# Three more up pairs by two by two steps in phase two, over sums read back from DRAM

## The chip, the cores and the metric

One NeuronCore of a Trainium2 chip. The metric is the device time of one execution in microseconds, as the median of several runs.

## The reference

One layer of a streaming encoder over 512 positions of width 1024, float32, and a last RMSNorm. Only the channel mixer at the end matters here:

```python
h = rms_norm(x, norm_ffn_g)
up = causal_dwconv(h @ w_up, conv_ffn_w)      # 1024 -> 2 x 2816, three taps along the sequence
a, b = split(up, 2)
x = x + (silu(a) * b) @ w_down                # 2816 -> 1024
return rms_norm(x, norm_f_g)
```

Before it the layer computes the input projections, a gated short convolution, a forgetting attention, sigmoid gates (`gates`), and a product with `w_o` (Wo).

## The kernel before, in words

Everything lies transposed: features on the partitions, the 512 positions along the free axis. A product in full float32 is made of three passes: each operand is split into a high part (ScalarE copies into a reduced-precision type: `wh`, `gh`, `x1h`) and a low part (VectorE subtracts: `wl`, `gl`, `x1l`), and TensorE adds high x high, low x high and high x low. Weights come chunk by chunk through SP's queue in the order of the list `stream`; `split` makes the next chunk's two parts one chunk ahead, into two buffers each, so a split waits for TensorE's end of the chunk before the last.

The hidden width has 22 blocks of 128. A **pair** j is block j of `a` and block j of `b`. A plain pair is two products of 8 inner blocks x 2 halves of the positions x 3 passes, 96 matmuls of 256 columns. A pair in `SUP` goes **by two by two steps** (`seven`): the two outputs, two inner blocks and two halves of positions form two by two matrices, multiplied with seven products instead of eight. For each of the four q (two inner blocks each) there are a chunk P (three weight forms, from the host) and a chunk F (four forms). The weight sums of F are made in DRAM beforehand by `make_forms`: a copy on SP's queue, an accumulating DMA on GpSimd's, and so on in six stages, set off one by one by `slot()` calls. On the side of the positions, four sums per q are needed (`up_forms`): `scale` and `sums` make them in the tile `y` (one buffer, from pool `gx`), `parts_of` splits them into slots `XF` and on of `gh` and `gl`. In before they are made in the Wo stage, and used for pairs 1, 2 and 5. `merge` puts the seven products together on VectorE. `up_form` hands TensorE the operands: g < 3 are parts of x, the others are forms; the chunk P already uses one form.

The mixer runs in two phases (`PHASES`): up pairs 0 to 11, then the down product over these (`STEPS[0]`, by two by two steps too, over `gh`/`gl` slots given by `place`), then pairs 12 to 21 and `STEPS[1]`, then a plain remainder and the tail (`fin_out`). `glu` multiplies the finished pair: `ge` (even j) and `go` (odd j) on GpSimd. `taps` is the convolution: one ScalarE operation and two on VectorE, into a tile `fu`. PSUM has eight banks; the output pair 2 of the down product stays open in four of them from phase one to the end of phase two (`HELD`). Short VectorE and ScalarE works are put in the list `later` and set between splits by `run_later` with a budget in microseconds, or forced by `flush`. Matmuls, DMAs and a few others keep the order in which the code is written; the rest is set by a scheduler.

Of the kernel before, what the change touches and what calls it, by code (L numbers as in the profile page):

```python
# [8 lines left out]
F32 = mybir.dt.float32  # L9
# [4 lines left out]
P = 128  # L14
D = 1024
S = 512
# [36 lines left out]
)  # L53
HELD = 2

# [5 lines left out]

SUP = (1, 2, 5)
XF = 26
UPD = tuple(((j, q), (j, q + 1)) for j in SUP for q in (0, 2))
DOUBLES = GATES + UPD + STEPS[0] + STEPS[1]
N0 = len(GATES) + len(UPD)
GROUPS = {"gate": (2, 4, 1), "up": (2, 4, 1), 0: (2, 4, 1), 1: (2, 3, 1)}


@with_exitstack  # L70
def block_kernel(ctx, tc, xT, vecs, wv, win, wmix, wo, wup, wst, wdp, outT):
# [70 lines left out]
    for ph, (j0, j1) in enumerate(PHASES):  # L142
        for j in range(j0, j1):
            if j in SUP:
# [44 lines left out]

    def make_forms(n0, n1, key):  # L190

        size, step, shift = GROUPS[key]
        make_forms.slot = 0
        cuts = [n0]
        for n in range(n0 + 1, n1 + 1):
            if n == n1 or n - cuts[-1] == size or len(DOUBLES[n]) != len(DOUBLES[cuts[-1]]):
                cuts.append(n)
        for g, (a, b) in enumerate(zip(cuts, cuts[1:])):
            m = len(DOUBLES[a]) * P
            f = dr.tile([P, b - a, 4 * m], F32, tag=f"f{a}", name=f"f{a}")  # L200
            w = wst[a:b].rearrange("n p c -> p n c")
            x0, x1, x2 = w[:, :, 3 * m : 5 * m], w[:, :, 5 * m : 7 * m], w[:, :, 7 * m : 8 * m]
            for n in range(a, b):
                made[n] = f[:, n - a, :]

            def put(dst, src):
                return lambda: keep(nc.sync.dma_start(dst, src))

            def add(dst, src):
                return lambda: keep(nc.gpsimd.dma_start(dst, src, accum_op=ALU.add))  # L210
# [3 lines left out]
            todo_bg.extend((make_forms.slot + step * k + shift * g, op) for k, op in enumerate(ops))  # L214
        todo_bg.sort(key=lambda w: w[0])
# [36 lines left out]
    def split(hl=None):  # L252
# [31 lines left out]
        if any(("e",) in w[2] for w in later):  # L284
            run_later(k, {"u": 3.8, "P": 1.6, "F": 1.2}[nm[0]])
            return
# [498 lines left out]

    def seven(doubles, n0, sets, operand, goes_on=None, stays=None, done=None, of="q"):

# [13 lines left out]
        for n, (name, prods) in enumerate(todo):  # L801
# [5 lines left out]
            for c, i, (xh, xl), b, h in prods:  # L807
                if i not in open_:
# [4 lines left out]
                    open_[i][b][:, th[h]], (i, b), wh[:, cs], wl[:, cs], xh, xl,  # L813
                    (i, b) not in before and i != goes_on, (i, b) not in after and i != stays,
                ))
            passes(out, len(out))
            if name[0] == "F":
                for i in sorted({i for _, i, *_ in prods}):
                    if (i, 0) not in after and i != stays:
                        done(i, open_.pop(i), sets[i])  # L820
# [217 lines left out]

    def up_forms(q):

        y = gx.tile([P, 4, 2 * P], F32, tag="y", name=f"y{q}")
        b11, b12, b21, b22 = (y[:, i, :] for i in range(4))
        fs = slice(XF + 4 * q, XF + 4 * q + 4)

# [9 lines left out]
        def sums():  # L1054
            nc.vector.scalar_tensor_tensor(b22, b11, -1.0, b22, op0=ALU.mult, op1=ALU.subtract)
            nc.vector.scalar_tensor_tensor(b21, b22, -1.0, b21, op0=ALU.mult, op1=ALU.subtract)

        def parts_of():
            nc.scalar.activation(gh[:, fs, :], y, AF.Copy)
            nc.vector.tensor_sub(gl[:, fs, :], y, gh.bitcast(F32)[:, fs, :])  # L1060
# [4 lines left out]
    def up_form(q, g):  # L1065
# [3 lines left out]
        n = XF + 4 * q + (0, 3, 1, 2)[g - 3]  # L1069
        return gh[:, n, :], gl[:, n, :]  # L1070

    po = None
    make_forms(N0, N0 + len(STEPS[0]), 0)
    for j in range(KB):
# [11 lines left out]
        if j % 2:  # L1086
            up_forms(j // 2)
    hg.close()
# [17 lines left out]

    acc = turns(0, 1, *(2, 3, 4, 5) * 2, 6, 7, 0, 1, 2, 3, 4, 5)
    USETS = {1: (2, 3, 4, 5), 2: (6, 7, 0, 1), 5: (6, 7, 0, 1)}
    ssq3 = xp.tile([P, S], F32, tag="ssq", name="ssq3")

    def place(ph, q):
        return (q - PHASES[ph][0] // 2) * (NF + ph)

    def up(j, ph, rb2, pu=None):
# [6 lines left out]

        if j in SUP:
            c = len(GATES) + 2 * SUP.index(j)
            slot()
            seven(
                UPD[c - len(GATES) :][:2], c, {j: USETS[j]}, up_form, of="x",
                done=lambda i, banks, ids: merge(ph, j, banks, ids, rb2, tap, uu),
# [163 lines left out]
    for ph, (j0, j1) in enumerate(PHASES):  # L1291
        if ph:
            flush()
            acc = turns(*X * 5)
        if ph:
            make_forms(N0 + len(STEPS[0]), len(DOUBLES), ph)
        for j in range(j0, j1):
# [14 lines left out]
        seven(  # L1312
            STEPS[ph], N0 + ph * len(STEPS[0]), ({0: X, 1: Y, 3: X, 2: Y}, {0: X, 1: Y, 2: Y})[ph],
            lambda q, g: (gh[:, place(ph, q) + g, :], gl[:, place(ph, q) + g, :]),
            goes_on=HELD if ph == 1 else None, stays=HELD if ph == 0 else None,
            done=lambda i, banks, ids: combine(ph, i, banks, ids),
# [59 lines left out]
    def fin_out(t, rc):  # L1376
        hs = halves[t]
        pb = rstd_bc(rc, 2, (1, 5)[t], f"n3{t}")[:, : S // 2]
        rs = fp.tile([P, S], F32, tag="fu", name=f"rs{t}", bufs=3)[:, : S // 2]
        nc.scalar.activation(rs, pb, AF.Copy)  # L1380
        for g, (a, b) in enumerate(((0, 1), (1, 3), (6, 8), (3, 5), (5, 6))):
            y = x1[:, a:b, hs]
            eng, r = (nc.gpsimd, rs) if g == 2 else (nc.vector, pb)
            eng.tensor_mul(y, y, r.unsqueeze(1).to_broadcast([P, b - a, S // 2]))  # L1384
            keep((nc.sync, nc.scalar)[g % 2].dma_start(outT[:, a:b, hs], y))
# [30 lines left out]
def _layout(i):  # L1416
# [45 lines left out]
    wu4 = wup.reshape(2 * NP, P, KB, P)  # L1462
    for w4, d in [(wga, d) for d in GATES] + [(wu4, d) for d in UPD] + [(wdn, d) for d in STEPS[0] + STEPS[1]]:
        def pick(*which):
# [44 lines left out]
```

## Time and profile before

| | us |
|---|---|
| median of 3 runs (lowest to highest) | 697.87 (697.65 to 698.26) |
| the profiled execution's own time | 698.61 |
| its span | 696.8 |
| TensorE busy | 686.7 (99%) |
| VectorE, ScalarE, GpSimd busy | 530.9, 359.7, 180.7 |

The page gives the busy time of each engine, the chain of work that ended last, and the costliest groups. In the timeline a row is start, duration, engine, line, operation, and in brackets the idle time before it with what ended it. The up pairs of phase one begin at 340.6 us, the down steps of phase one at 471, phase two at 527.4, its down steps at 636.2.

### The profile page before, as it was taken

The numbers are of one execution on the slowest core, as the hardware profiler recorded it, in microseconds if no ns is written. First come the engines' busy times: TensorE is split into PE (matmuls) and PEld (weight loads), VectorE is DVE, ScalarE is ACT, GpSimd is POOL, SyncE is SP. The second block draws the span as 40 slices with busy tenths as digits, with TensorE's granted clock in tenths as the row PEclk, the third lists the DMA queues.
The fourth block names the chain that finished last, engine by engine and source line by source line (L and its number), as shares of the span: only waits on it lengthen the run. The fifth ranks groups of instructions, "written<-read, shape, count | busy, mean of one in ns | idle before, by whom it ended". The sixth has DMA issues, their size and how long they took to land.

```text
span 696.8 us, 14636 instructions
## 1 busy us (share of the span) xinstructions
PE 686.7 (99%) x5972; PEld 684.9 (98%) x5972; DVE 530.9 (76%) x824; ACT 359.7 (52%) x567; POOL 180.7 (26%) x196
## 2 busy tenths in 40 slices
PE   9999999999999999999999999999999999999996
PEld 9999999999999998999999999999999999999995
DVE  6677877776678776868869799988674677878793
ACT  5665655645565443446554455465443344445572
POOL 4134847532211201113523143210000313221001
PEclk9999999999999999999999999999999999999998
DMA  7528978542688687666799775536646686676513
GB/s 253 161 70 276 205 183 201 121 91 89 234 237 257 183 234 208 202 216 141 110 316 296 199 184 130 153 124 193 198 129 228 143 192 162 184 170 175 156 31 121
DMA packets 58387, 124.68 MB, mean 179 GB/s; under 512 B 5280, under 2 KB 26800, under 8 KB 58320
## 3 DMA queue, kind: packets, MB, share of 16 engines
q1 hardware_dynamic: 40776, 99.68, 44.0%
q0 software_dynamic: 16304, 22.88, 20.6%
q10 hardware_dynamic: 1240, 1.19, 0.5%
q8 instruction: 47, 0.77, 0.4%
q14 instruction: 20, 0.16, 0.1%
HBM read 121.57 MB, written 39.32 MB: 231 GB/s over the span
## 4 chain that ended last, share of the span: by engine, by line
PE 58%; DVE 2%; DMA 0%; ACT 0%; issue 0%; DVEq 0%; ACTq 0%
PE p_up L308 21%; PE dn L326 19%; PE p_up L326 7%; PE p_wo L308 6%; PE pdB L308 1%; PE pdA L308 1%; PE ya L308 1%; PE yc L308 1%; DMA raw_dp<-in_wdp_dram 0%; PE pc_n L343 0%; DVE fu L562 0%; DVE fu L565 0%; PE pb_n L362 0%; DVE gl L1231 0%; DVE wl_up L278 0%; DVE x L1384 0%
## 5 line engine op out<-in xcount | busy, mean ns | idle before, releaser
L308 PE MATMUL p_up<-x1h,wh_up 128*128 128x256 f32 x464 | 90.5, 276 | 0.0
L308 PE MATMUL p_up<-x1l,wh_up 128*128 128x256 f32 x464 | 90.3, 276 | 0.0
L308 PE MATMUL p_up<-x1h,wl_up 128*128 128x256 f32 x464 | 90.3, 276 | 0.0
L210 POOL DMA_DIRECT2D f<-in_wst_dram x57 | 66.1, 1311 | 15.6 <-DMA f<-f 15.3
L308 PEld LDWEIGHTS p_up<-x1h,wh_up 128*128 128x128 f32 x464 | 69.9, 188 | 0.0
L308 PEld LDWEIGHTS p_up<-x1l,wh_up 128*128 128x128 f32 x464 | 69.9, 188 | 0.0
L308 PEld LDWEIGHTS p_up<-x1h,wl_up 128*128 128x128 f32 x464 | 69.8, 188 | 0.0
L274 ACT ACTIVATE wh_up<-raw_up 128x1024 fp32r<-128x1024 f32 x38 | 40.2, 1058 | 55.8 <-PE p_up L308 46.2
L278 DVE TENSOR_TENSOR wl_F<-raw_F,wh_F 128x1024 fp32r<-128x1024 f32 (+1 forms) x36 | 46.9, 1304 | 17.8 <-ACT wh_F L274 17.8
L278 DVE TENSOR_TENSOR wl_up<-raw_up,wh_up 128x1024 fp32r<-128x1024 f32 x38 | 48.3, 1270 | 12.8 <-ACT wh_up L274 12.7
L308 PE MATMUL p_in<-xgh,wh_in 128*128 128x256 f32 x288 | 56.8, 279 | 0.0
L308 PE MATMUL p_in<-xgh,wl_in 128*128 128x256 f32 x288 | 56.6, 278 | 0.0
L308 PE MATMUL p_in<-xgl,wh_in 128*128 128x256 f32 x288 | 56.5, 278 | 0.0
L274 ACT ACTIVATE wh_F<-raw_F 128x1024 fp32r<-128x1024 f32 (+1 forms) x36 | 37.9, 1052 | 34.1 <-PE dn L326 26.6
L1204 POOL TENSOR_TENSOR ge<-fu,fu 128x512 f32<-128x512 f32 x11 | 17.6, 1602 | 138.6 <-DVE fu L565 119.1
L274 ACT ACTIVATE wh_P<-raw_P 128x768 fp32r<-128x768 f32 (+1 forms) x36 | 30.0, 834 | 31.4 <-PE dn L326 22.6
L308 PEld LDWEIGHTS p_in<-xgh,wh_in 128*128 128x128 f32 x288 | 44.7, 188 | 0.7
L326 PE MATMUL dn<-gh,wh_F 128*128 128x256 f32 x192 | 45.1, 276 | 0.0
L326 PE MATMUL dn<-gl,wh_F 128*128 128x256 f32 x192 | 45.1, 276 | 0.0
L278 DVE TENSOR_TENSOR wl_P<-raw_P,wh_P 128x768 fp32r<-128x768 f32 (+1 forms) x36 | 34.5, 958 | 13.6 <-ACT wh_P L274 9.0
L308 PEld LDWEIGHTS p_in<-xgl,wh_in 128*128 128x128 f32 x288 | 43.7, 188 | 0.0
L308 PEld LDWEIGHTS p_in<-xgh,wl_in 128*128 128x128 f32 x288 | 43.6, 188 | 0.0
(351 smaller groups left out, 2154.8 us busy)
## 6 DMA issues: line engine op xcount, KB each, us to landing
raw_up<-in_wup_dram SPq DMA_DIRECT2D x38, 512.0 KB, 3.9
raw_F<-f SPq DMA_DIRECT2D x35, 512.0 KB, 4.9
raw_P<-in_wst_dram SPq DMA_DIRECT2D x35, 384.0 KB, 4.7
raw_in<-in_win_dram SPq DMA_DIRECT2D x26, 512.0 KB, 3.5
f<-in_wst_dram POOLq DMA_DIRECT2D x35, 256.0 KB, 6.4
f<-in_wst_dram SPq DMA_DIRECT2D x17, 512.0 KB, 5.5
f<-in_wst_dram POOLq DMA_DIRECT2D x17, 512.0 KB, 8.1
f<-f SPq DMA_DIRECT2D x34, 256.0 KB, 5.6
```

What stands on the lines that cost most here:

```text
L210: return lambda: keep(nc.gpsimd.dma_start(dst, src, accum_op=ALU.add))
L274: ins = nc.scalar.activation(hi, raw, AF.Copy)
L278: ins = nc.vector.tensor_sub(lo, raw, hi.bitcast(F32))
L308: keep(nc.tensor.matmul(out[:, cs], w, x[:, cs], start=start and i == 0 and c == 0, stop=stop and i == 2 and c == len(cut) - 1,))
L326: keep(nc.tensor.matmul(out, wl if x == 1 else wh, xl if x == 2 else xh, start=opens and bk not in seen, stop=closes and bk not in left,))
L1204: keep(nc.gpsimd.tensor_mul(ge, a.rearrange(halves_of, h=2), b.rearrange(halves_of, h=2)))
```

## The change

- `SUP` holds the pairs of each phase: 1, 3, 5 in phase one (1, 2, 5 before), and 14, 16, 18 in phase two (none before). Their banks are always 2 to 5 (`USET`).
- `up_forms(q, 0)` writes each `y` to the DRAM tile `ys` as well, on GpSimd's queue. `up_forms(0, 1)`, at the start of phase two, loads `y` back; its `parts_of` calls `up_forms(q + 1, 1)`, so the four loads follow each other through the one buffer `y`.
- Pair 2 of the down product isn't held in PSUM: it is added into `x1` at the end of each phase, and `seven` loses `goes_on` and `stays`.
- `make_forms` takes a start, and the forms of the new pairs are made in phase one. In the gates stage the three `slot()` calls of an iteration stand together at its beginning. `place` gives other slots in phase two. The last up block of each phase calls `split_next()` once. The budget "u" is 4.2 instead of 3.8.
- The tail multiplies all output blocks on VectorE; ScalarE's copy `rs` and GpSimd's share go.

```diff
-SUP = (1, 2, 5)
-XF = 26
+SUP = ((1, 3, 5), (14, 16, 18))
+XF = (26, 0)
...
-                    (i, b) not in before and i != goes_on, (i, b) not in after and i != stays,
+                    (i, b) not in before, (i, b) not in after,
...
-    make_forms(len(GATES), N0, "up")
+    make_forms(NU[0], ND[0], "up0")
     for j in range(KB):
         gs = []
-        slot()
+        for _ in range(3):
+            slot()
...
         for pp, hh, ll, o in ((yc, ych, ycl, 0), (ya, oth, otl, 4)):
-            slot()
...
-    def up_forms(q):
-
-        y = gx.tile([P, 4, 2 * P], F32, tag="y", name=f"y{q}")
+    ys = dr.tile([4, P, 4, 2 * P], F32, tag="ys", name="ys")
+
+    def up_forms(q, ph):
+
+        y = gx.tile([P, 4, 2 * P], F32, tag="y", name=f"y{ph}{q}")
...
+            keep(nc.gpsimd.dma_start(ys[q], y))
+
         def parts_of():
             nc.scalar.activation(gh[:, fs, :], y, AF.Copy)
             nc.vector.tensor_sub(gl[:, fs, :], y, gh.bitcast(F32)[:, fs, :])
-
+            if ph and q < 3:
+                up_forms(q + 1, ph)
+
+        if ph:
+            keep(nc.gpsimd.dma_start(y, ys[q]))
+            later.append((len(parts) + 1, 1.25, (("x", q),), parts_of))
+            return
...
+    make_forms(NU[1], ND[1], "up1", 10)
...
-    acc = turns(0, 1, *(2, 3, 4, 5) * 2, 6, 7, 0, 1, 2, 3, 4, 5)
-    USETS = {1: (2, 3, 4, 5), 2: (6, 7, 0, 1), 5: (6, 7, 0, 1)}
+    acc = turns(0, 1, 6, 7, 0, 1, 6, 7, 0, 1, 2, 3, 6, 7, 0, 1, 2, 3)
+    USET = (2, 3, 4, 5)
...
+            if i and j + 1 == PHASES[ph][1]:
+                split_next()
...
         if ph:
-            flush()
-            acc = turns(*X * 5)
-        if ph:
-            make_forms(N0 + len(STEPS[0]), len(DOUBLES), ph)
+            acc = turns(6, 7, 0, 1, 6, 7, 0, 1, 6, 7, 0, 1, 6, 7)
+            up_forms(0, 1)
+            make_forms(ND[1], len(DOUBLES), ph)
...
-        rs = fp.tile([P, S], F32, tag="fu", name=f"rs{t}", bufs=3)[:, : S // 2]
-        nc.scalar.activation(rs, pb, AF.Copy)
-        for g, (a, b) in enumerate(((0, 1), (1, 3), (6, 8), (3, 5), (5, 6))):
+        for g, (a, b) in enumerate(((0, 1), (1, 3), (3, 5), (5, 7), (7, 8))):
```

GpSimd's queue in the gates stage, before and then now. `ga` is the sum of the two gated branches of an output block, `f10` to `f14` are the weight forms of the up pairs of phase one.

```order
L977 TENSOR_TENSOR ga4_3349<-ga4_3349,gb4_3354 128x512
L210 DMA f14_2593<-in_wst_dram 256x1x256
L977 TENSOR_TENSOR ga5_3538<-ga5_3538,gb5_3543 128x512
L210 DMA f10_2591<-in_wst_dram 256x1x256
L977 TENSOR_TENSOR ga6_3728<-ga6_3728,gb6_3733 128x512
```

```order
L978 TENSOR_TENSOR ga4_3351<-ga4_3351,gb4_3356 128x512
L978 TENSOR_TENSOR ga5_3540<-ga5_3540,gb5_3545 128x512
L211 DMA f10_2591<-in_wst_dram 256x1x256
L978 TENSOR_TENSOR ga6_3729<-ga6_3729,gb6_3734 128x512
L211 DMA f12_2592<-in_wst_dram 256x1x256
```

The accumulating DMA of `f14` stood ahead of `ga5` and now stands behind it.

GpSimd's queue at the start of phase two, before and then now. `ge6` and `go6` are the products of pairs 12 and 13, `f28` (before) and `f34` (now) are the first weight forms of phase two's down steps, and `y10` to `y13` are the four sums loaded back, the second digit being q.

```order
L1204 TENSOR_TENSOR ge5_6099<-fu100_6088,fu101_6094 128x512
L1204 TENSOR_TENSOR ge6_7007<-fu120_6940,fu121_7002 128x512
L210 DMA f28_6883<-in_wst_dram 256x1x512
L1211 TENSOR_TENSOR go6_7135<-fu130_7067,fu131_7130 128x512
L210 DMA f30_6884<-in_wst_dram 256x1x512
```

```order
L1218 TENSOR_TENSOR ge5_6068<-fu100_6057,fu101_6063 128x512
L1070 DMA y10_6913<-ys_4002 128x1024
L1218 TENSOR_TENSOR ge6_7045<-fu120_6972,fu121_7040 128x512
L211 DMA f34_6915<-in_wst_dram 256x1x512
L1070 DMA y11_7123<-ys_4002 128x1024
L1225 TENSOR_TENSOR go6_7181<-fu130_7109,fu131_7176 128x512
L211 DMA f36_6916<-in_wst_dram 256x1x512
L1070 DMA y12_7193<-ys_4002 128x1024
L1070 DMA y13_7263<-ys_4002 128x1024
```

The loads of y11 and y12 stand behind the products of pairs 12 and 13, and y13 right behind y12.

VectorE at the same place, before and then now: `fz121` is the evacuation of pair 12's second half, the rows into `fu121` its two taps, `wl` the low parts of weights.

```order
L1139 TENSOR_TENSOR fz121_7000<-p_up25_6951,rb_n2_4669 128x512
L278 TENSOR_TENSOR wl_up27_7076<-raw_up27_6849,wh_up27_7075 128x1024
L562 SCALAR_TENSOR_TENSOR fu121_7002<-fz121_7000,vec_64,fu121_7002 128x511
L565 SCALAR_TENSOR_TENSOR fu121_7002<-fz121_7000,vec_64,fu121_7002 128x510
L1139 TENSOR_TENSOR fz130_7065<-p_up26_7016,rb_n2_4669 128x512
L278 TENSOR_TENSOR wl_up28_7142<-raw_up28_6945,wh_up28_7141 128x1024
```

```order
L1153 TENSOR_TENSOR fz121_7038<-p_up25_6989,rb_n2_4675 128x512
L279 TENSOR_TENSOR wl_up27_7118<-raw_up27_6875,wh_up27_7117 128x1024
L563 SCALAR_TENSOR_TENSOR fu121_7040<-fz121_7038,vec_64,fu121_7040 128x511
L1065 TENSOR_TENSOR gl_3998<-y10_6913,gh_3997 128x1024
L566 SCALAR_TENSOR_TENSOR fu121_7040<-fz121_7038,vec_64,fu121_7040 128x510
L1153 TENSOR_TENSOR fz130_7107<-p_up26_7058,rb_n2_4675 128x512
L279 TENSOR_TENSOR wl_P28_7188<-raw_P28_6977,wh_P28_7187 128x768
L563 SCALAR_TENSOR_TENSOR fu130_7109<-fz130_7107,vec_64,fu130_7109 128x511
L566 SCALAR_TENSOR_TENSOR fu130_7109<-fz130_7107,vec_64,fu130_7109 128x510
L1065 TENSOR_TENSOR gl_3998<-y11_7123,gh_3997 128x1024
```

The split of y10 into `gl` stands between the two taps, that of y11 behind the taps of pair 13's first half. On TensorE the chunk P of pair 14 is now six products of three matmuls: x in the first four of each q's group, the form in the last two, so the low part of y11 is read by the twelfth matmul of the first chunk, and that of y12 and y13 by the sixth and the twelfth of the second.

More of the change, by code (lines that the diff above doesn't have):

```diff
@@ L60 @@
 PCUTS = (0, 8, 12, 20)
[L62 to L67 removed]
+SUP = ((1, 3, 5), (14, 16, 18))
+XF = (26, 0)
+UPD = tuple(tuple(((j, q), (j, q + 1)) for j in js for q in (0, 2)) for js in SUP)
+DOUBLES = GATES + UPD[0] + STEPS[0] + UPD[1] + STEPS[1]
+NU = [len(GATES), len(GATES + UPD[0] + STEPS[0])]
+ND = [NU[i] + len(UPD[i]) for i in range(2)]
+GROUPS = {"gate": (2, 4, 1), "up0": (2, 4, 1), "up1": (2, 3, 1), 0: (2, 4, 1), 1: (2, 3, 1)}
 @with_exitstack
@@ L188, in block_kernel, with make_forms @@
     made, todo_bg = {}, []
-    def make_forms(n0, n1, key):
+    def make_forms(n0, n1, key, start=0):
         size, step, shift = GROUPS[key]
-        make_forms.slot = 0
+        if not start:
+            make_forms.slot = 0
         cuts = [n0]
@@ L213, in make_forms @@
             ops = (put(f0, x0), add(f0, x1), put(f1, f[:, :, :m]), add(f1, x1[:, :, m:]), put(f2, f1), add(f2, x2))
-            todo_bg.extend((make_forms.slot + step * k + shift * g, op) for k, op in enumerate(ops))
+            todo_bg.extend((start + step * k + shift * g, op) for k, op in enumerate(ops))
         todo_bg.sort(key=lambda w: w[0])
@@ L818, in seven @@
                 for i in sorted({i for _, i, *_ in prods}):
-                    if (i, 0) not in after and i != stays:
+                    if (i, 0) not in after:
                         done(i, open_.pop(i), sets[i])
```

33 lines of the change are left out of this document (15 added, 18 removed).

## The prediction

> **What bounds the kernel now.** I read the page first, then TensorE's table of waits, then the chain that ended last.
>
> ```profile
> span 696.8 us, 14636 instructions
> PE 686.7 (99%) x5972; PEld 684.9 (98%) x5972; DVE 530.9 (76%) x824; ACT 359.7 (52%) x567; POOL 180.7 (26%) x196
> ```
>
> TensorE is busy for all but 10.1 us of its span. Its table of waits (who was waited for: us in total, times, longest) names 3.5 of these; most of the rest is the tail after the last matmul.
>
> ```profile
> PE dn L326 <- ACT wh_P L274: 1.6, 1, 1.6
> PE warm L115 <- DVE ones L107: 1.1, 1, 1.1
> PE dn L326 <- DVE wl_P L278: 0.8, 1, 0.8
> ```
>
> In the chain (start, us, what) a plain up block is 48 matmuls in 1.36 + 4.08 = 5.44 us:
>
> ```profile
> 527.39 1.36 PE p_up L326 x12
> 528.75 4.08 PE p_up L308 x36
> ```
>
> So a matmul of 256 columns costs 4.08/36 = 0.1133 us, and a matmul saved is time saved, but any new wait of TensorE adds to the time in full.
>
> **Part 1: fewer matmuls, -4.08 us.** A plain pair has 96 matmuls, a pair by two by two steps 84 (4 blocks of inner dimension x 7 products x 3). Three more such pairs save 36, x 0.1133 = 4.08 us. Moving the three of phase one from 1, 2, 5 to 1, 3, 5 changes no count; ending pair 2's sum in phase one changes none either. It adds a second `combine` on VectorE, six operations no wider than the 512 columns of a tap (0.74, below), so 4.4 us at most, beside pairs 12 and 13, where VectorE was busy for 11.2 of 21.6 us (a window's row: length, then PE, PEld, DVE, ACT and POOL busy, granted clock, DMA share, GB/s); without that cover they would delay the splits by as much.
>
> ```profile
> 527.40:549.00 21.60, 21.60 (x193) 21.60 (x193) 11.21 (x13) 6.48 (x9) 2.29 (x2) 1.00 0.62 163
> ```
>
> **Part 2: two old waits go, -1.55 and -0.78 us.** The first lies in the gates stage (timeline rows of POOL, ACT and PE):
>
> ```profile
> 267.84 1.04 POOL L210 DMA_DIRECT2D f<-in_wst_dram  x1 [15.29 <-DMA f<-f]
> 268.44 1.76 POOL L977 TENSOR_TENSOR ga<-ga,gb 128x512 f32<-128x512 f32 x1
> 270.24 0.63 ACT L978 ACTIVATE mh<-ga 128x512 fp32r<-128x512 f32 x1 [3.75 <-POOL ga L977]
> 270.77 0.83 ACT L274 ACTIVATE wh_P<-raw_P 128x768 fp32r<-128x768 f32 x1
> 271.65 0.38 PE L326 MATMUL dn<-xgh,wh_P 128*128 128x256 f32 x1 [1.55 <-ACT wh_P L274]
> ```
>
> GpSimd's queue stands 15 us at an accumulating DMA whose input copy has not landed; `ga5` is behind it, ScalarE's `mh` behind that, and the next weight split behind `mh`. In the new order `ga5` stands ahead of that DMA, so I take the whole 1.55 us as gone (bounds: 0, if another transfer takes its place, to 1.55). The second is the split of the first down chunk, which VectorE does only after the last `gl`:
>
> ```profile
> 469.12 1.28 DVE L1231 TENSOR_TENSOR gl<-go,gh 128x512 fp32r<-128x512 f32 x2
> 470.32 0.95 DVE L278 TENSOR_TENSOR wl_P<-raw_P,wh_P 128x768 fp32r<-128x768 f32 x1
> ```
>
> The added `split_next()` puts this split ahead of the `gl` rows; the 0.8 us go (bounds 0 to 0.8).
>
> **Part 3: the sums kept in DRAM, +20.7 us.** Writing `ys` in the Wo stage lies beside TensorE: the next `scale` may start about a microsecond late, and blocks there are 5.44 us long with a split made one block ahead. Reading them back is another matter. All four pass through the one buffer `y`: load, ScalarE's copy into `gh`, VectorE's difference into `gl`, and only then the next load. Prices of a hop: four 512 KB loads from GpSimd (issue ns min/median/max, then us to landing), and the two splits of the same tile in the Wo stage:
>
> ```profile
> L856 POOL DMA_DIRECT2D xt<-in_xT_dram x4: 555/559/639, 185.7 to 187.4; - x4
> DMA to landing us min/median/max: 4.9/6.1/7.5
> L1059 ACT ACTIVATE gh<-y x4: 1062/1062/1063, 313.5 to 346.5; 128x1024 fp32r<-128x1024 f32 x4
> L1060 DVE TENSOR_TENSOR gl<-y,gh x4: 1224/1226/1226, 314.6 to 347.6; 128x1024 fp32r<-128x1024 f32 x4
> ```
>
> No row shows such a load alone on the queue; I take 5.5 us to landing, between the burst's first and its median, since an accumulating transfer goes ahead of two of them (bounds below). A hop is then 5.5 + 1.06 + 1.23 = 7.8 us, and three follow the first. Where they start is read from the same place of before, the first pairs of phase two; t counts from TensorE's start of pair 12, 527.39:
>
> ```profile
> 538.31 1.06 ACT L274 ACTIVATE wh_up<-raw_up 128x1024 fp32r<-128x1024 f32 x1 [0.95 <-PE p_up L308]
> 539.40 1.23 DVE L278 TENSOR_TENSOR wl_up<-raw_up,wh_up 128x1024 fp32r<-128x1024 f32 x1 [0.40 <-ACT wh_up L274]
> 540.54 0.74 DVE L562 SCALAR_TENSOR_TENSOR fu<-fz,vec,fu 128x511 f32<-128x511 f32 x1
> 539.27 0.71 ACT L561 ACTIVATE fu<-fz,vec 128x512 f32<-128x512 f32 x1
> 542.25 1.29 POOL L1204 TENSOR_TENSOR ge<-fu,fu 128x512 f32<-128x512 f32 x1 [75.93 <-DVE fu L565]
> 543.48 1.06 POOL L210 DMA_DIRECT2D f<-in_wst_dram  x1
> ```
>
> The first tap of pair 12's second half starts at t = 13.15. In the new order VectorE makes the first `gl` (y10) between the two taps, done at 13.15 + 0.7 + 1.2 = 15.0, and the second tap at 15.8; GpSimd's `ge6`, at 14.9 before, waits for it. The load of y11 stands behind `ge6` (1.23 to the next start) and the accumulation of f34 (1.06): issued at 18.1, landed 23.6, `gl` done 25.9. Pair 14 begins at 4 x 5.44 = 21.76, and its first chunk already needs y11 in its twelfth matmul, at 23.0: **2.9 us wait**.
>
> The chunk ends at 26.7 (7 matmuls more). ScalarE's split of the next P chunk waits for it (0.83), then comes the tap of pair 13's second half (0.71), then on VectorE a tap, a split and the last tap (0.74, 0.95, 0.74): 30.6. GpSimd's `go6` needs that tap (1.29, as `ge`), then f36 (1.06), and only behind both stands the load of y12: issued 32.9, landed 38.4, `gl` done 40.7. TensorE has done its F chunk (24 matmuls, 2.7) by 29.4 and needs y12's low part at 30.0: **10.7 us wait**. The load of y13 waits for that `gl`: landed 46.2, `gl` done 48.5, while TensorE wants it six matmuls after y12, at 41.4: **7.1 us wait**. Together 20.7. Behind VectorE's and ScalarE's waiting instructions stand the splits of pair 15's weights; TensorE wants them only 31 matmuls (3.5 us) later, and they take 1.06 + 1.23, so nothing is added; behind the load of y13 on GpSimd's queue stand only three accumulations for phase two's steps and `ge7`, which comes after pair 14.
>
> At landings of 4.9 the sum falls by 1.8, at 7.5 it rises by 6. A 512 KB load from SP, another queue, has a median of 3.9 on the page:
>
> ```profile
> raw_up<-in_wup_dram SPq DMA_DIRECT2D x38, 512.0 KB, 3.9
> f<-in_wst_dram POOLq DMA_DIRECT2D x17, 512.0 KB, 8.1
> ```
>
> That is a lower end, 3 x 1.6 = 4.8 less. The Trainium skill, "DMA: Bandwidth & Descriptors", "Anatomy of one DMA — SWDGE (gpsimd) path", gives 2.0 us plus bytes/436e3 per DMA, an estimate of 3.2 for 512 KB, by which the 20.7 would be 13.8; the burst's fastest, 4.9, speaks against it here.
>
> **Part 4: TensorE's clock after the long waits, +2.0 us.** The granted clock (third from the end of a window's row) falls soon after the last matmul:
>
> ```profile
> 689.57 0.61 PE L362 MATMUL pb_n<-ident,rc_n 128*128 128x128 f32 x4
> 691.50:692.00 0.50, 0.00 (x0) 0.00 (x0) 0.50 (x2) 0.00 (x0) 0.50 (x1) 1.00 0.03 10
> 692.00:692.50 0.50, 0.00 (x0) 0.00 (x0) 0.50 (x2) 0.00 (x0) 0.01 (x1) 0.69 0.72 252
> 692.50:693.00 0.50, 0.00 (x0) 0.00 (x0) 0.15 (x1) 0.00 (x0) 0.00 (x0) 0.50 0.66 219
> ```
>
> Two microseconds idle and it is at half. At the span's start, two matmuls of 256 columns take 0.43 us from 5.50 to the next start, twice the 0.23 of later; the rate is reached at about 5.9:
>
> ```profile
> 1.05 4.21 PE L115 MATMUL warm<-ones 128*128 128x128 f32 x18 [1.05 <-DVE ones L107]
> 5.50 0.63 PE L474 MATMUL pb<-wh_v,xgh 128*128 128x256 f32 x2
> 5.93 0.49 PE L472 MATMUL pa<-wh_v,xgh 128*128 128x264 f32 x2
> ```
>
> From 1.05 to 5.9 are 4.8 us at half speed, 2.4 lost; the wait for y13 hides what is lost before it, so the loss counts once. I take 2.0 (bounds 0 to 2.4). "TensorE: Matmul & The Clock Gate", "What's actually happening", in the Trainium skill puts the way back at about 3.4 us of work, which would make it 1.7.
>
> **Part 5: the tail, +0.2 us.**
>
> ```profile
> 690.28 0.38 ACT L1380 ACTIVATE rs<-pb_n 128x256 f32<-128x256 f32 x1 [1.06 <-PE pb_n L362]
> 690.70 1.95 DVE L1384 TENSOR_TENSOR x<-x,pb_n 128x256 f32<-128x256 f32 x4 [1.28 <-ACT rs L1380]
> ```
>
> VectorE starts 0.4 sooner (no `rs`), but multiplies 8 blocks instead of 6: 1.95/6 x 2 = 0.65 more. The last output goes 0.2 later (bounds -0.4 to +0.65).
>
> **The sum** against the profiled execution's own 698.61: - 4.08 - 1.55 - 0.78 + 20.7 + 2.0 + 0.2 = 715.1. The median shown, 697.87, lies 0.74 under it: 714.4.
>
> **The rivals.**
> Loads land soon (chance 0.17): alone on the queue they need what SP's need, 3.9 us. 714.4 - 4.8 = 709.6, and 707.6 if the clock isn't lost. For it: the 4.9 comes from a burst of four. Against: y11 and y12 follow accumulations.
> Loads land late (0.13): y11 and y12 queue behind transfers that took 8.1 in the median, and y13 meets pair 15's weights: 7.5 each, 714.4 + 6 = 720.4.
> The loads are hidden (0.05), the side of faster: all land before they are needed, and the time is 714.4 - 22.7 = 691.7. The point from which it decides: from y10's `gl` (t = 15.0) to y13's need without waits (4 x 5.44 + 4.76 + 1.25 = 27.8) are 12.8 us for three hops, so 4.3 each and at most 2.0 to landing, even if GpSimd's `go6` were not in between. No 512 KB row is near that.
> VectorE becomes the bound in phase two (0.05): pairs by steps want more of it, and it would lag through pairs 15 to 19. The densest stretches of phase one speak against it (DVE is the third busy time):
>
> ```profile
> 373.00:394.00 21.00, 21.00 (x188) 21.00 (x187) 17.40 (x27) 8.25 (x13) 7.79 (x7) 1.00 1.03 265
> 416.00:438.00 22.00, 22.00 (x197) 22.00 (x196) 21.77 (x35) 12.62 (x20) 5.53 (x4) 1.00 0.62 135
> ```
>
> Even at 21.8 of 22 us TensorE never waited there. If it did, some 1 us per step pair: 714.4 + 3 = 717.4.
>
> **How the numbers follow.** The forecast of 714.4 has 0.60. The range goes from 705.5 (early landings, 707.6, and 2 us less for splits that overlap better than counted) to 721.5 (late landings and 1 us of other waits); it leaves out the hidden case and the far ends. A difference within 0.2% (about what a measurement of this kernel can tell from no change) lies between the hidden case and the rest, where no case is: 0.01. Faster 0.05, slower 0.94.
>
> **What would show it.** Right: TensorE's waits list `dn` in pair 14 behind `gl` of line 1065, two or three waits of 3, 11 and 7 us; GpSimd's `y` loads start at t = 18, 33 and 41; 36 fewer matmuls; no 1.6 us wait for `wh_P` at the gates. Wrong: TensorE unbroken through pair 14, or `y` loads landing within 2 us.

## The result, and the profile after

The changed kernel takes 738.31 us in the median (737.07 to 740.97, four runs) against 697.88: a ratio of 1.0577 [1.0557, 1.0598]. Slower, as forecast, but 24 us over the forecast of 714.4 and outside its range. The profiled execution has 738.93 us and a span of 737.1, 40.3 more than before.

The page (engine, busy time, instructions; then the granted clock in 40 slices):

```profile
span 737.1 us, 14705 instructions
PE 696.3 (94%) x5936; PEld 692.3 (94%) x5936; DVE 553.4 (75%) x858; ACT 369.4 (50%) x579; POOL 194.3 (26%) x211
PEclk9999999999999999999899999999997689999998
```

The 36 matmuls are gone (5972 to 5936), and yet TensorE is busy 9.6 us longer: about 13.7 us of its busy time are matmuls at a low clock (9.6 and the 4.1 of the 36). TensorE's waits in the changed kernel:

```profile
PE dn L327 <- ACT gh L1064: 21.6, 3, 11.0
PE pc_n L344 <- POOL ssq L1003: 3.0, 1, 3.0
PE p_up L327 <- ACT wh_up L275: 2.8, 1, 2.8
PE dn L327 <- DVE wl_F L279: 2.5, 1, 2.5
PE dn L327 <- DVE gl L1065: 2.0, 3, 0.7
...
PE p_up L309 <- DVE wl_up L279: 0.8, 1, 0.8
PE dn L327 <- ACT wh_F L275: 0.7, 1, 0.7
```

Both old waits, for `wh_P` at the gates and `wl_P` at the end of phase one, are gone. The first and fifth rows are the chain through `y`, 23.6 us; the others were not forecast. What each place costs, wait and slow clock together, is seen by counting matmuls in stretches of 15 us (length, TensorE busy and matmuls, granted clock, DMA share, GB/s):

```profile
330.00:345.00 15.00, 14.20 (x124) 1.00 0.76 122
345.00:360.00 15.00, 12.01 (x80) 0.77 0.91 245
375.00:390.00 15.00, 14.29 (x127) 1.00 1.07 260
390.00:405.00 15.00, 12.88 (x99) 0.89 0.95 271
420.00:435.00 15.00, 15.00 (x135) 1.00 0.85 135
555.00:570.00 15.00, 7.93 (x59) 0.76 0.54 131
570.00:585.00 15.00, 4.77 (x29) 0.73 0.63 150
585.00:600.00 15.00, 8.64 (x47) 0.61 0.72 147
675.00:690.00 15.00, 12.46 (x97) 0.89 0.36 111
```

A full stretch has 135, so I count a missing matmul as 15/135 = 0.111 us. That gives a ledger of the whole loss:

| place | missing | us | forecast |
|---|---|---|---|
| the loads of `y`, 555 to 600 | 270 | 30.0 | 22.7 |
| end of the Wo stage, 330 to 360 | 64 beyond before | 7.1 | 0 |
| weights of phase one, 375 to 405 | 44 | 4.9 | 0 |
| first down steps, 480 to 495 | 9 | 1.0 | 0 |
| end of phase two, 675 to 690 | 38 | 4.2 | 0 |

Together 47.2; less 4.1 for the matmuls, 1.55 and 0.78 for the old waits and 0.4 for the tail, 40.4: the spans differ by 40.3. That it closes so well is in part luck. A matmul that reaches over an end of a stretch is counted too (20 us hold 179, not 180), so a missing one is nearer the 0.1133 of the prediction, and the old waits counted in the same way are 27 missing matmuls before (17 in 270 to 285, 10 in 465 to 480), 3.1 us. So priced the sum is 48.2 - 4.1 - 3.1 - 0.4 = 40.6, which still leaves little out.

Of the 24 us over the forecast, 7.3 lie in the first row and 17.2 in the four rows with a forecast of 0; the tail gives 0.6 back.

The chain through `y`, from the timeline, the summary of the tile, and the chain that ended last:

```profile
565.93 1.06 ACT L1064 ACTIVATE gh<-y 128x1024 fp32r<-128x1024 f32 x1 [7.79 <-DMA y<-ys]
572.84 1.61 POOL L1225 TENSOR_TENSOR go<-fu,fu 128x512 f32<-128x512 f32 x1 [16.32 <-DVE fu L566]
574.99 1.03 POOL L1070 DMA_DIRECT2D y<-ys  x1
584.70 1.06 ACT L1064 ACTIVATE gh<-y 128x1024 fp32r<-128x1024 f32 x1 [6.72 <-DMA y<-ys]
DMA to landing us min/median/max: 3.7/6.5/10.4
593.96 5.21 PE dn L327 x31
```

`go6` holds up the load of y12, as forecast; the load, issued at 574.99, lands 9.7 later. The load of y11 took 10.4, that of y13, with no accumulation ahead, 4.2. The 31 matmuls behind the last wait take 5.21 us and not 3.5.

The end of the Wo stage:

```profile
343.35 0.73 ACT L1051 ACTIVATE y<-x,vec 128x512 f32<-128x512 f32 x1 [2.98 <-DMA ys<-y]
345.80 0.61 ACT L1002 ACTIVATE sq<-x 128x512 f32<-128x512 f32 x1
346.56 1.51 POOL L1003 TENSOR_TENSOR ssq<-ssq,sq 128x512 f32<-128x512 f32 x1 [3.50 <-ACT sq L1002]
348.12 1.86 PE L344 MATMUL pc_n<-ones,ssq 128*128 128x1 f32 x8 [3.00 <-POOL ssq L1003]
```

The next `scale` stands 3 us until the copy of `y` to DRAM has landed. Behind it on ScalarE stand a weight split, `x1h` and the last square; `ssq`, the sum of squares for the norm, waits for the square, and TensorE's norm waits for `ssq`. Each passes the 3 us on.

The weights of phase one, and the end of phase two:

```profile
391.01 1.06 ACT L275 ACTIVATE wh_up<-raw_up 128x1024 fp32r<-128x1024 f32 x1 [5.76 <-DMA raw_up<-in_wup_dram]
raw_up<-in_wup_dram SPq DMA_DIRECT2D x32, 512.0 KB, 5.2
677.87 1.22 DVE L279 TENSOR_TENSOR wl_F<-raw_F,wh_F 128x1024 fp32r<-128x1024 f32 x1
679.14 2.08 PE L327 MATMUL dn<-gh,wl_F 128*128 128x256 f32 x8 [2.54 <-DVE wl_F L279]
```

A weight load has a median of 5.2 us over the whole kernel where it was 3.9. At the end VectorE comes to `wl_F` only after taps and `gl` rows of pairs 20 and 21.

### The profile page after: what moved, and what is told of

It reads as the page before. It is cut to its first block, busy times and chain, and to the rows that moved or that the text cites. A ratio compares the mean times of both kernels' runs of the same rounds, so it can differ in the third digit from the quotient of the medians.

```text
span 737.1 us, 14705 instructions
## 1 busy us (share of the span) xinstructions
PE 696.3 (94%) x5936; PEld 692.3 (94%) x5936; DVE 553.4 (75%) x858; ACT 369.4 (50%) x579; POOL 194.3 (26%) x211
## 5 line engine op out<-in xcount | busy, mean ns | idle before, releaser
L309 PE MATMUL p_up<-x1h,wl_up 128*128 128x256 f32 x392 | 77.3, 279 | 0.8 <-DVE wl_up L279 0.8
L309 PE MATMUL p_up<-x1h,wh_up 128*128 128x256 f32 x392 | 77.7, 280 | 0.0
L309 PE MATMUL p_up<-x1l,wh_up 128*128 128x256 f32 x392 | 77.2, 278 | 0.0
L309 PEld LDWEIGHTS p_up<-x1h,wl_up 128*128 128x128 f32 x392 | 60.1, 191 | 1.0 <-DVE wl_up L279 1.0
L1218 POOL TENSOR_TENSOR ge<-fu,fu 128x512 f32<-128x512 f32 x11 | 17.2, 1562 | 165.5 <-DVE fu L566 128.0
L309 PEld LDWEIGHTS p_up<-x1h,wh_up 128*128 128x128 f32 x392 | 60.2, 191 | 0.0
L309 PEld LDWEIGHTS p_up<-x1l,wh_up 128*128 128x128 f32 x392 | 59.9, 190 | 0.0
L279 DVE TENSOR_TENSOR wl_up<-raw_up,wh_up 128x1024 fp32r<-128x1024 f32 x32 | 43.5, 1361 | 19.4 <-ACT wh_up L275 17.2
L327 PE MATMUL dn<-gh,wh_P 128*128 128x256 f32 x141 | 35.8, 287 | 21.6 <-ACT gh L1064 21.6
L327 PE MATMUL dn<-gh,wh_F 128*128 128x256 f32 x228 | 55.3, 281 | 0.7 <-ACT wh_F L275 0.7
L327 PE MATMUL dn<-gl,wh_F 128*128 128x256 f32 x228 | 55.0, 280 | 0.0
L279 DVE TENSOR_TENSOR wl_P<-raw_P,wh_P 128x768 fp32r<-128x768 f32 (+1 forms) x42 | 41.3, 982 | 15.4 <-ACT wh_P L275 10.7
L327 PEld LDWEIGHTS dn<-gh,wh_P 128*128 128x128 f32 x141 | 27.3, 193 | 22.4 <-ACT gh L1064 22.3
```

The source lines that it names most:

```text
L279: ins = nc.vector.tensor_sub(lo, raw, hi.bitcast(F32))
L309: keep(nc.tensor.matmul(out[:, cs], w, x[:, cs], start=start and i == 0 and c == 0, stop=stop and i == 2 and c == len(cut) - 1,))
L327: keep(nc.tensor.matmul(out, wl if x == 1 else wh, xl if x == 2 else xh, start=opens and bk not in seen, stop=closes and bk not in left,))
L1218: keep(nc.gpsimd.tensor_mul(ge, a.rearrange(halves_of, h=2), b.rearrange(halves_of, h=2)))
```

## Experiments

Ratios are to runs of the kernel before on the same chip. My theory was that the chain is the 30 us and that the four unforeseen places come from three other parts of the change: the copies to DRAM, the making of the new weight sums, VectorE's load. The rival was that the reordered rest of the change, or slow loads whatever the chain, cost as much.

### plain2: no pairs by steps in phase two

```diff
-SUP = ((1, 3, 5), (14, 16, 18))
+SUP = ((1, 3, 5), ())
...
-            keep(nc.gpsimd.dma_start(ys[q], y))
...
-            up_forms(0, 1)
```

> Pairs 14, 16 and 18 are plain again; their forms, the copies of the sums to DRAM and back are gone; all else of the change stays (pairs 1, 3, 5, no pair held over, reordered sums, split, tail). Theory (all that was lost over the forecast comes with the three pairs of phase two: the chain through y, the next scale waiting for the copy of y to DRAM, the copies that make their forms beside phase one, VectorE's backlog at the end): 697.9 - 1.55 - 0.78 + 0.2 = 695.8. Rival (the reordered rest costs by itself: the losses of 5.9 us in 345 to 360, 4.9 in 375 to 405 and 4.2 in 675 to 690 stay, only the 30 us in 555 to 600 go): 695.8 + 15 = 711.

Measured 695.3 us, 0.9963 [0.9951, 0.9975]: the theory's time, and the fastest kernel of all here, 43 us under the changed one. Besides the one at the span's start TensorE has one wait left, at 374.9 in phase one:

```profile
PE dn L327 <- DVE wl_P L279: 0.9, 1, 0.9
```

So the reordered sums, the split, the tail and pairs 1, 3, 5 bring the 2.1 us forecast for them, and cost no more than that; everything lost comes with the pairs of phase two.

### loads_sp and nochain: the queue, and the buffer

```diff
 # loads_sp
-            keep(nc.gpsimd.dma_start(y, ys[q]))
+            keep(nc.sync.dma_start(y, ys[q]))
 # nochain
+        y = gl.bitcast(F32)[:, fs, :] if ph else gx.tile(...)
...
+            for q in range(4):
+                up_forms(q, 1)
```

> One word changed: the four loads of y are issued on SP's queue and not on GpSimd's; the one buffer stays. Theory (two of the three long landings are time spent behind accumulating transfers on GpSimd's queue, and the issue waits for GpSimd's go and its accumulations): y11 is issued when the first gl is done, t = 15, lands in 4.2, and hops take 6.5; only y13 is late, by some 3 us; 738.3 - 30 + 4 = 712. Rival (the hop costs the same on any queue, as the DMA engines are shared, or SP's queue stands at weight loads that wait for a buffer): 733 to 740.

> The sums are read straight into their places in gl, all four loads issued on GpSimd at the start of phase two; ScalarE and VectorE split them there, one per chunk. The one buffer between DRAM and gl is gone, the work of the engines and the bytes are the same. Theory (the chain through one buffer costs the 30 us, wait and slow clock): 738.3 - 30 = 708. Rival (the loads themselves are slow on that queue, 10 us each one after the other): y13 lands 40 us after the start and is wanted at 31: 9 us of wait and 2 of clock stay, 719.

On SP's queue: 725.5 us, 1.0395 [1.0374, 1.0416], between the two. The waits for `gh` and `gl` fall to 13.2. The loads of y11 and y12, and the copies that wait for them:

```profile
552.24 0.33 SPq L1070 DMA_DIRECT2D y<-ys  x1
555.58 1.06 ACT L1064 ACTIVATE gh<-y 128x1024 fp32r<-128x1024 f32 x1 [0.58 <-DMA y<-ys]
557.98 0.33 SPq L1070 DMA_DIRECT2D y<-ys  x1
563.20 1.06 ACT L1064 ACTIVATE gh<-y 128x1024 fp32r<-128x1024 f32 x1 [1.30 <-DMA y<-ys]
```

They land in 3.3 and 5.2 us, though the accumulations still run on GpSimd's queue. But y13, issued only after y12's `gl`, lands 8.3 us after its issue, among the weights: another queue shortens the hops and leaves the chain.

Without the chain: 714.6 us, 1.0237 [1.0215, 1.026]. The place is nearly whole, 11 matmuls missing and not 270:

```profile
555.00:570.00 15.00, 14.39 (x124) 1.00 0.69 176
645.00:660.00 15.00, 7.94 (x57) 0.77 0.21 66
620.00:640.00 20.00, 20.00 (x179) 20.00 (x179) 19.02 (x29) 10.40 (x15) 7.45 (x7) 1.00 0.87 222
```

Shown: the chain, not the loads as such, makes the 30 us; four loads set off together land in 6.6 in the median and are in time. But only 23.7 us came back. The second row is the end of phase two: 78 missing, 8.7 us, where it was 38. The third (PE, PEld, DVE, ACT, POOL) shows VectorE busy for 19.0 of 20 us ahead of it, but the changed kernel has 18.6 of 20 at the same place (655 to 675). What differs is the work between `wl_P` and `wl_F`:

```profile
639.29 0.95 DVE L279 TENSOR_TENSOR wl_P<-raw_P,wh_P 128x768 fp32r<-128x768 f32 x1
652.82 1.21 DVE L279 TENSOR_TENSOR wl_F<-raw_F,wh_F 128x1024 fp32r<-128x1024 f32 x1
```

That is 12.6 us, against 8.0 in the changed kernel. That the long waits had let VectorE catch up there is the likely reason; no run shows it.

### alone: no accumulations among the loads

```diff
-            make_forms(ND[1], len(DOUBLES), ph)
+            make_forms.slot = 0
+            make_forms(ND[1], len(DOUBLES), ph, 8)
```

(with one slot between the stages, not three.)

> The changed kernel with the weight sums for the down steps of phase two made from pair 16 on, so that no accumulating transfer stands on GpSimd's queue among the four loads of y; the one buffer stays. Theory (landings of 10.4 and 9.7 us come from accumulating transfers ahead on that queue, and 4.2 is the price of a load alone): y11 lands about 21 us after pair 12's start and costs 0.5 us of wait, y12 some 8, y13 some 6, together 14 to 15 and not 23.7: 738.3 - 9 = 729. Rival (a load takes 10 us there whatever stands ahead, or the order of go decides): 736 to 738.

The step that was mis-sized, the landing, is confirmed. The loads of y11 and y13, issued at 556.25 and 575.55, are waited for until:

```profile
559.94 1.06 ACT L1064 ACTIVATE gh<-y 128x1024 fp32r<-128x1024 f32 x1 [2.99 <-DMA y<-ys]
579.18 1.06 ACT L1064 ACTIVATE gh<-y 128x1024 fp32r<-128x1024 f32 x1 [5.19 <-DMA y<-ys]
PE p_up L327 <- ACT wh_up L275: 11.8, 3, 4.6
```

They land in 3.7 and 3.6, y12 in 5.3, and TensorE's waits for `gh` and `gl` are 12.5 us, not 23.6. All the same the kernel took 744.6 us, 1.0671 [1.0642, 1.0699]: the making of the sums, moved to pair 16 and on, now crowds the weights of the up blocks there, where two of the last row's three waits lie. The time theory was wrong because I priced only what the move took away.

### filler and filler2: the clock

```diff
+FILL = {f"P{NU[1]}": {10: 45}, f"P{NU[1] + 1}": {4: 80, 10: 25}}
...
+            for _ in range(fill.get(n, 0)):   # as in filler2
+                keep(nc.tensor.matmul(todo[0][0][0], zc[:, :1].to_broadcast([P, P]), x1h[:, 0, : 2 * P], start=False, stop=False))
```

> The changed kernel with 150 more matmuls of 256 columns with zero weights, which add nothing: 45 ahead of the first wait for y11's parts, 80 ahead of y12's, 25 ahead of y13's (5.1, 9.1 and 2.8 us, each shorter than the wait it lies in). Theory (30.0 us are lost in 555 to 600, of which 23.7 are waits and the rest is matmuls at a low clock, because TensorE stood still): the clock stays up, and some 5 us come back: 733. Rival (those matmuls are slow for another reason, such as weights that come late): no gain, 738 or more.

> The same 150 matmuls with zero weights as in the filler run, but the column of zeros lies in space that was unused, so that every other tile keeps its address: in the filler run matmuls were some 3% slower all along the kernel (130 to 132 in 15 us, not 135), also 250 us ahead of the first added one, where its only difference is that column, which shifts the tiles. Theory of the clock: 733 (30.0 us lost in 555 to 600 become 25), and 135 matmuls in 15 us elsewhere. Rival (the matmuls after the waits are slow for another reason): 738 or more. If 130 to 132 in 15 us appear again, the shift was not their cause.

These are 45, 80 and 25 matmuls ahead of the first use of y11, y12 and y13. The first kernel took 743.5 us, 1.065 [1.0604, 1.0696], with matmuls slower along much of the kernel; with the zeros in unused space 735.3, 1.0528 [1.0498, 1.0558]. So with 150 matmuls more the kernel took 3.0 us less. The two intervals just meet, so the time alone shows little; the clock and the count show it. From 557 to 600, of the changed kernel and of filler2:

```profile
557.00:600.00 43.00, 19.34 (x116) 17.77 (x115) 14.98 (x20) 11.96 (x15) 6.55 (x7) 0.68 0.65 149
557.00:600.00 43.00, 37.93 (x301) 37.14 (x300) 18.76 (x27) 11.90 (x16) 6.25 (x7) 0.92 0.69 163
```

The clock rises from 0.68 to 0.92; the place costs 25.9 us (322 matmuls of which 150 are filler, so 233 missing) and not 30.0. The slow matmuls come from the waits.

### nowrite: no copies to DRAM

```diff
-            keep(nc.gpsimd.dma_start(ys[q], y))
...
+            keep(nc.gpsimd.dma_start(y, xT[:, 2 * q : 2 * q + 2, :]...))
```

> The changed kernel without the four copies of y to DRAM; the loads in phase two read the input x instead (the same bytes), so pairs 14, 16 and 18 compute something else. Theory (the copy that the next scale waits for makes the wait for ssq; the transfers for the weight sums of pairs 14, 16, 18 make the waits of 375 to 405): the 1.2 us of 330 to 345 and the 5.9 of 345 to 360 go, the rest stays: 731. Rival (the copies also delay the weights in phase one): the 4.9 us of 375 to 405 go too, 726.

Measured 733.5 us, 1.0505 [1.0478, 1.0531]. The wait for `ssq` is gone and 330 to 360 has its full count: the copies make that loss. The weights' waits stay, moved earlier and no smaller (13 and 43 missing, 6.2 us):

```profile
375.00:390.00 15.00, 12.39 (x92) 0.89 1.06 309
```

### parts, parts_noforms, parts_steps, steps_nowrite: the transfers of phase one

```diff
 # parts, and the loads straight into gh and gl
-            keep(nc.gpsimd.dma_start(ys[q], y))
+            keep(nc.gpsimd.dma_start(yh[q], gh.bitcast(F32)[:, fs, :]))
+            keep(nc.gpsimd.dma_start(yl[q], gl.bitcast(F32)[:, fs, :]))
 # parts_noforms, in make_forms
+            if key == "up1":
+                continue
...
 # parts_steps
-    make_forms(NU[1], ND[1], "up1", 10)
+        if not ph:
+            make_forms(NU[1], ND[1], "up1")   # just ahead of the down steps
...
 # steps_nowrite: the copies only for q == 0, and all loads read these
```

> Kept in DRAM are the split parts, copied out of gh and gl in the Wo stage and read straight back into gh and gl at the start of phase two, eight loads on GpSimd: twice the bytes, no work of ScalarE or VectorE in phase two, and the copy to DRAM no longer reads y, so the next scale doesn't wait for it. Theory: 738.3 - 30.0 (555 to 600) - 5.9 (345 to 360) - 1.2 (330 to 345) = 701; the losses in 375 to 405 (4.9) and 675 to 690 (4.2) stay. Rival (bytes decide: eight loads of 512 KB at 5 us on one queue land 40 us after the start, 9 us late): 712; and the copies out crowd the Wo stage.

> The kernel with the split parts kept in DRAM (705.7), without the copies and accumulations that make the weight sums of pairs 14, 16 and 18 in phase one: the chunks are loaded from the unsummed weights instead, so these pairs compute something else; loads and work of the engines stay. Theory (the waits for weights of up blocks in phase one come from these transfers): the 84 matmuls missing in 360 to 480 (9.3 us) come back: 696.4; the 4.7 us at the end of phase two stay. Rival (the copies of the parts to DRAM in the Wo stage, or the reordered pairs 1, 3, 5, make them): 705 stays.

> The same kernel (705.7) with the weight sums of pairs 14, 16 and 18 made during the down steps of phase one, one transfer per chunk, where the DMA share was 0.5 to 0.7, and not from pair 1 on, where it was 1.0 and more. Theory (these transfers crowd the weights of the up blocks): as in the run without them, 700.6, if they do not crowd the loads of the steps. Rival (they wait on one another wherever they are, and pair 14's chunks come late): a new wait in pair 14 of some us, 705 or more.

> The kernel with split parts in DRAM and the weight sums made in the down steps (699.8), with only the first two of the eight copies of the parts to DRAM; all eight loads of phase two read these two, so pairs 14, 16 and 18 compute something else. Theory (the copies out, landing in 330 to 375, make what is left of the weights' waits there): the 34 matmuls missing in 360 to 390 (3.8 us) come back, 696.0; the 29 missing at the end of phase two stay. Rival (the copies land without crowding anything): 699 to 700.

Keeping the parts: 705.7 us, 1.0109 [1.0093, 1.0125]; the chain and the `ssq` wait are gone, but 360 to 480 now lacks 90 matmuls, where the changed kernel lacks 45. Without the making of the sums 700.6, 1.0036 [1.0023, 1.005]; with the sums made in the down steps 699.8, 1.0029 [1.0014, 1.0044]; with six of the eight copies out left away too 696.7, 0.9987 [0.9973, 1.0001]. So on this base the making of the sums costs 5 to 6 us and six of the copies out 3; where the DMA share was 0.5 to 0.7 the same sums cost next to nothing. The wait at the first down steps goes with the sums too: 465 to 480 lacks 10 in parts, and none without them or with them made later. The only large gap left in the last one is the end of phase two, 38 missing of 135:

```profile
630.00:645.00 15.00, 12.46 (x97) 0.89 0.29 89
```

### parts_two, parts_dve, parts_split, hp2: the end of phase two

```diff
 # parts_two
+SUP = ((1, 3, 5), (14, 16))
 # parts_dve: pairs 19 to 21 without the last tap
 # parts_split
+        while ph and len(parts) < chunk.n + 2:
+            split()
         flush((("e",),))
 # hp2: y in hp with bufs=2, the sums 4 slots later, and
+            (nc.gpsimd if ph else nc.vector).tensor_sub(gl[:, fs, :], y, ...)
```

> The same kernel with split parts (705.7), with pair 18 plain again: two pairs of phase two by steps. Theory (VectorE, busy for 56 of 60 us there, is behind at the end of phase two, and the merge of pair 18 comes last): the 4.7 us there go, 12 matmuls come back (1.4), and a third fewer transfers in phase one bring up to 3 us: 699 to 702.4. Rival (the backlog is that of the whole phase, and pairs 14 and 16 leave it): the wait for wl_F stays at 2 to 3 us, 703 to 706.

> The kernel with split parts kept in DRAM (705.7), without the last tap in the six halves of pairs 19 to 21: 6 x 0.74 = 4.4 us less for VectorE near the end of phase two, and those taps are missing from the output. Theory (VectorE is behind there, and what it still owes delays wl_F): the wait for wl_F and the slow matmuls behind it go, 4.7 us: 701. Rival (wl_F waits for its own weights or for ScalarE): 705 to 706.

> The kernel with split parts kept in DRAM (705.7), with one thing moved: at the end of phase two the first F chunk is split ahead of the owed work of pairs 20 and 21, not behind it. No work is taken away. Theory (the order of the instructions makes the wait at the end of phase two: the split stands in VectorE's and ScalarE's rows behind all that pairs 19 to 21 still owe, which is why leaving out taps changed nothing): the 4.7 us there go, 701. Rival (VectorE has more work than time there): the wait comes back at the next chunks or at the evacuations, 704 to 706.

> Sums read straight into gl, as in the run without the chain, and three more edits: y has two buffers in the Wo stage (in space that is free there), so that scale needn't wait for the copy to DRAM; the difference that makes gl in phase two is taken by GpSimd, not VectorE; the weight sums of pairs 14, 16, 18 start four slots later. Theory: 691.5 for the fewer matmuls and the two old waits gone, plus what is left of the weights' waits in phase one (3 to 5) and at phase two's end (2 to 4): 697 to 700. Rival (GpSimd at about half VectorE's speed delays ge, go and the accumulations behind them): 703 to 708.

Two pairs: 701.5 us, 1.0049 [1.0034, 1.0064]; 23 matmuls missing from 615 to 675, where parts lacks 44. Without six taps: 705.1, 1.0087 [1.006, 1.0114], no gain that stands out; the 2.5 us wait is now for ScalarE's `wh_F`, behind other work in that kernel's order, so this run doesn't settle what the amount does. Splitting early: 710.9, 1.0183 [1.0166, 1.02], slower by 5. The wait came back behind the first chunk, for `wl_P` and `gl`, 82 missing:

```profile
645.00:660.00 15.00, 11.29 (x71) 0.77 0.30 87
660.00:675.00 15.00, 13.64 (x117) 1.00 0.39 120
```

The order alone does not cure it: what is pushed back is needed soon too. GpSimd as helper: 713.2, 1.0208 [1.0174, 1.0241], and a wait of 7.0 for `wl_F`, as long as the 7.1 of nochain: what was taken off VectorE brought nothing. A reason stands in the timeline of hp2, GpSimd's `gl` beside VectorE:

```profile
557.31 5.40 POOL L1065 TENSOR_TENSOR gl<-gl,gh 128x1024 fp32r<-128x1024 f32 x2 [5.39 <-ACT gh L1064]
557.64 2.87 DVE L566 SCALAR_TENSOR_TENSOR fu<-fz,vec,fu 128x510 f32<-128x510 f32 x1
560.43 3.36 DVE L279 TENSOR_TENSOR wl_F<-raw_F,wh_F 128x1024 fp32r<-128x1024 f32 x1
```

A tap of 0.74 takes 2.87 and a split of 1.22 takes 3.36: VectorE stands still while GpSimd computes.

### best1, best2, four: can it be made to pay?

```diff
 # best1: nochain + y in hp with bufs=2 + sums made in the down steps + early split
 # best2: the same with SUP = ((1, 3, 5), (14, 16))
 # four: plain2 with
+SUP = ((1, 2, 4, 6), ())
```

> All cures together: sums read straight into gl (no chain), y with two buffers in the Wo stage (no wait of scale), weight sums made in the down steps of phase one, the first F chunk of phase two split ahead of the owed work. Theory (the four places are all that was lost): 697.9 - 4.1 - 1.6 - 0.8 = 691.5, and 1 to 3 us of small waits: 692.5 to 694.5. Rival (VectorE, which also splits the sums in phase two, has more work than time there): 697 to 702.

> The same with two pairs of phase two by steps, 14 and 16, pair 18 plain. Theory: 12 matmuls more than with three, 692.9 and the same small waits: 694 to 696. Rival (VectorE has more work than time): it has less here than with three, so this one is the faster of the two, 695 to 698.

> The kernel with pairs of phase two plain (695.3), with four pairs of phase one by steps, 1, 2, 4 and 6, and not three: 12 matmuls fewer. Theory (TensorE's matmuls are the time as long as VectorE keeps up): 695.3 - 1.36 = 693.9. Rival (VectorE, at 21.8 of 22 us in the densest stretch of before, cannot take some 4.5 us more for a fourth pair, two extra splits of 0.95 and 2.7 us of merging): a wait for a split of 2 to 4 us, 696 to 698.

All cures together: 711.5 us, 1.0195 [1.0177, 1.0213], and with two pairs 705.5, 1.0103 [1.0085, 1.0121]. The rival held, and more: with the splits of the sums on VectorE and the early split, 127 matmuls are missing at the end of phase two, 14 us. A fourth pair in phase one: 697.7, 0.9993 [0.9981, 1.0005], 2.4 slower than three, its 1.4 us more than eaten by one wait and the clock behind it:

```profile
PE p_up L327 <- DVE wl_up L279: 2.5, 1, 2.5
```

The end of phase two by the number of pairs: none in plain2, 2.6 us with two (parts_two), 4.9 with three (parts; 3.8 in parts_steps), 8.7 with three and the splits of the sums as well (nochain). That this work makes the loss is shown; how much of it is VectorE's amount and how much the alternation of ScalarE and VectorE in what pairs 19 to 21 owe is open.

## Why the prediction was right or wrong

**Part 1, 36 matmuls:** right, the count is exact.

**Part 2, the two old waits:** right; neither row is there after, and plain2 gives 2.8 us for them, the tail and what else is reordered, against 2.1. In the changed kernel itself a wait of 0.7 for `wh_F` stands in the first down steps instead, and goes with the sums.

**Part 3, the chain:** the mechanism was right: three waits for `gh` (line 1064) and `gl` (line 1065), y12 behind `go6`, y13 behind y12's `gl`. Pair 12 starts at 537.76 (527.39 before, and the rows there come 10.37 later), and the loads are issued at t = 17.7, 37.2 and 49.6, where the forecast had 18, 33 and 41. The sum was 23.6, not 20.7, single waits 7.1, 11.7 and 4.9 for 2.9, 10.7 and 7.1. The mis-sized step is the landing, 5.5 for each: it is 3.6 to 5.3 without accumulations on the queue (alone), 10.4 and 9.7 behind one. An accumulation ahead isn't the only cause of a late landing: y13 on SP's queue took 8.3 without one. I had named the late landing as a rival, with 7.5 for all three; behind an accumulation it was more, alone less. The estimate for a load from the Trainium skill's figures ("DMA: Bandwidth & Descriptors", "Anatomy of one DMA — SWDGE (gpsimd) path"), 3.2, is near what a load alone showed, 3.6; it does not hold behind an accumulation.

"Lies beside TensorE" was the step that failed outright. I granted the next `scale` a microsecond of lateness, but 3 us came, and what stands behind `scale` on ScalarE leads to `ssq`, where the next stage begins and no block covers it: 7.1 us.

**Part 4, the clock:** mis-sized, 2.0 for some 6 us in 555 to 600. I let it count once, since the last wait would hide earlier losses. But by the order of the instructions the work that issues the next load stands behind splits that wait for TensorE, so its slow matmuls lengthen the chain. By the rows the excess over 0.1133 us a matmul is 2.9 us after y11, 1.2 after y12, 2.0 after y13. The 2.0 for one is what the trace shows, and near the estimate of 1.7 from the window of about 3.4 us in the Trainium skill ("TensorE: Matmul & The Clock Gate", "What's actually happening"); each of the three waits pays it again, and shorter ones can pay some of it (0.77 in 345 to 360 with a wait of 3.0). They don't always: the same wait of 2.5 for `wl_F` left the clock at 1.00 in parts_steps and at 0.89 in steps_nowrite, 29 and 38 missing.

**Part 5, the tail:** 0.4 saved where I had 0.2 lost, within its bounds.

**Not in the sum at all:** the transfers for the sums of pairs 14, 16 and 18. I listed the accumulations of phase two, and gave the new ones in phase one no term and no reason for none. They cost 5 to 6 us in parts, and their place in the changed kernel 4.9.

**The rivals:** "VectorE becomes the bound in phase two" (0.05, 3 us) names the place of a loss that came beside the forecast, 4.2 us at the end of the phase, and 8.7 once the chain is cured, which is why 23.7 us came back and not 30. That these pairs' work makes it is shown; that VectorE's amount of work alone does is not. The rows I held against it, 21.8 of 22 us without a wait, came from phase one, with plain pairs behind; in phase two the owed work meets the down steps.

## What to carry to other kernels

Price a copy "beside" the work by following, on its engine, everything behind the instruction that waits for it to the next place where a stage begins. Count a transfer's landing with what stands ahead of it on its queue, and a long wait of TensorE with the clock behind it. Where a second engine is near full, an edit that saves a little on the busiest one and gives the second more to do can lose even when its waits are cured one by one. Here the best kernel with the three pairs that leaves nothing out took 699.8 us (parts_steps), and the one without them 695.3.

## What the hardware showed

In hp2, GpSimd's differences of 2.7 us stopped the VectorE operations beside them (0.74 to 2.87 us for a tap, 1.22 to 3.36 for a split). The Trainium skill says so of VectorE operations with two SBUF inputs beside a GpSimd operation that reads SBUF ("SBUF — State Buffer", "SBUF: two separate sides"), an exclusive lock for the whole instruction, and the trace agrees.

A column of zeros put among the small constants, which shifts the tiles behind it, went with 129 to 132 matmuls in 15 us in many stretches, at a granted clock of 1.00, against 135 when it lay in unused space (filler, then filler2):

```profile
420.00:435.00 15.00, 15.00 (x129) 1.00 0.76 208
420.00:435.00 15.00, 15.00 (x135) 1.00 0.81 130
```

Other stretches of the same run had 135, and parts_noforms, on the same chip as filler, had 135 in 420 to 435 too. What exactly a tile's place does to a matmul's rate stays open.
